# Two query groups of the second attention moved between the last projection blocks; both key halves from one product

## The chip, the cores and the metric

The kernel runs on one core of one Trainium2 chip. The metric is the device time of one execution in microseconds (us). An execution is a little longer than its span, which runs from the first to the last instruction of the profile. TensorE is called PE here, VectorE DVE, ScalarE ACT, GpSimd POOL, and SyncE (SP) is the queue from which nearly all DMAs are issued.

## What is computed

The reference is two transformer blocks in sequence on x of 2048 rows by 1024.

```
h  = rms_norm(x) * (1 + scale) + shift;  qa ka va fa za qb kb vb zb = h @ w_in
oa = forgetting_attention(8 heads of 64);  ob = sliding_window(rope(qb), rope(kb), 2 key heads)
x  = x + gate * rms_norm([oa * silu(za), ob * silu(zb)] @ w_out)
# second block, 16 meta tokens ahead of the sequence
q_a c_kv q_idx k_idx w_idx gate_a q_h f_h i_h gate_h = h @ w_in_2
a  = attention over the 256 best keys by an index score + the meta tokens, 8 heads, relative bias
r  = hgrn2(q_h, f_h, i_h)                  # recurrence over chunks of the sequence
y  = [a * silu(gate_a), rms_norm(r) * silu(gate_h)] @ w_out_2
out = layer_norm(2**0.25 * h + y)
```

## The kernel before

Products are made in float16 with a high and a low part (three products for one), and the program is written in a framework that orders the instructions of every engine ahead of time: program order gives each a priority, which `high_priority(offset=...)` shifts (a negative offset makes it less urgent), and a later instruction may be placed ahead of an earlier one that isn't ready. Once placed, every engine and the SP queue run their instructions in that order, each waiting in turn. Pools of tiles lie on a left or a right stack in SBUF; a pool that opens where another has closed waits, tile by tile, until the old tiles there have been read.

- `blocks1` makes the first projection. For the sliding keys and queries `rotated` computes, for each of 4 groups of 512 rows, two products `p[0]` and `p[1]` (the two halves of each head, m columns each; m is 64 for the keys `kb` and 128 for `qb`), and rotates them with DVE, POOL and ACT (L516 to L527). The first attention's heads run at the same time.
- `phase_proj2` makes the second projection (L1242 to L1444): index scores, latent keys and values, then the twelve blocks of `BLK2` in `stream`, where the weights of the next block are loaded and split while the current one is computed. A block `qa`, `qh` or `fh` is 8 banks of 24 products of 512 columns; a block `ga`, `gh` or `ih` 16 banks of 24 products of 256. Each bank is evacuated by ACT: Sigmoid for `fh`, Silu for `gh`, `ga` and `qh`, a copy for `qa` and `ih`. `bank()` hands out the PSUM banks in turn. `Quick.run` selects the 256 keys of each row, in three batches of row tiles (`QUICK`), on DVE and ACT, from scores in a tile `sc`, and writes the masks.
- `phase_dsa` (L1982 to L2225) then runs the second attention by query groups g of 512 rows: 8 heads each, and per head `prepare` (loads, row maxima from L2052 and L2058) and `main` (4g+4 key blocks and the meta block: products L2103 to L2115, then Exp, cast and subtraction in `Att.weights`, L746 to L752, then the products with the values, L776 to L778, three for each of the query tiles). Between the heads stand, by a count of key blocks `done`, the eight chunks of the recurrence (`CH`, `Hgrn.chunk`, one after another through single buffers) and the output product with the norm of each of 16 row tiles (`O2`, `out2`, `norm2`).

Group 0 has 5 steps a head, group 1 has 9, group 2 has 13 and group 3 has 17: 40, 72, 104 and 136 for eight heads, 352 in all.

## Time and profile before

| what | value |
|---|---|
| median of 3 runs | 3169.38 us (3162.87 to 3175.8) |
| profiled execution: time, span | 3170.48 us, 3168.7 us |
| mean granted TensorE clock | 0.938 of full speed |
| busy: PE, DVE, ACT, POOL | 2822.7, 2101.6, 1686.9, 1450.2 us |
| matmuls | 25152 |

A busy PE need not be at its peak, as matmuls overlap and their ends are modelled; where a product's price is wanted, the distance from one start to the next is read. The granted clock is given as a share of 2.4 GHz. Idle time of an engine that isn't the bound costs nothing.

### The profile page before, as it was taken

What the parts mean: (1) busy time and instruction counts of PE and PEld (TensorE: products, weight loads), DVE (VectorE), ACT (ScalarE), POOL (GpSimd) and SP (SyncE); (2) the same over time, 40 slices, a digit from 0 to 9 for tenths busy, and PEclk for the clock granted to TensorE, in tenths of its full rate; (3) what the DMA queues carried; (4) which work ended last, traced back from release to release, by engine and by line L of the source; (5) the groups of instructions that cost most, each with busy time, mean ns of one, the idle gap of its engine ahead of it and who ended that gap; (6) DMA issues with size and microseconds to landing.
All of it is one profiled execution on the core that took longest, in us unless ns stands there. A gap on an engine that the chain in (4) does not pass through costs nothing. (4 is left out here: it accounts for less than half of the span.)

```text
span 3168.7 us, 65862 instructions
## 1 busy us (share of the span) xinstructions
PE 2822.7 (89%) x25152; PEld 1858.8 (59%) x25152; DVE 2101.6 (66%) x5073; ACT 1686.9 (53%) x3058; POOL 1450.2 (46%) x1241
## 2 busy tenths in 40 slices
PE   7899999999997899999998889899678888988997
PEld 5554444477884555544445665358566566666663
DVE  7523765566678676646499699830578778888763
ACT  4423665576566655634356466321455456657763
POOL 3211446564333555534233433610456567768752
PEclk9899999999996799999999989899679989999998
DMA  6222343532235343334433532222753444443331
GB/s 235 82 87 84 105 129 111 173 95 69 79 94 167 109 142 108 124 91 157 111 97 101 160 125 73 89 91 63 182 159 102 137 133 113 118 117 110 122 97 59
DMA packets 271184, 364.28 MB, mean 115 GB/s; under 512 B 60205, under 2 KB 192033, under 8 KB 269705
## 3 DMA queue, kind: packets, MB, share of 16 engines
q1 hardware_dynamic: 270424, 359.96, 37.8%
q8 instruction: 199, 3.26, 0.4%
q14 instruction: 129, 1.05, 0.1%
q10 hardware_dynamic: 432, 0.02, 0.0%
HBM read 247.05 MB, written 112.82 MB: 114 GB/s over the span
## 5 line engine op out<-in xcount | busy, mean ns | idle before, releaser
L752 POOL TENSOR_TENSOR plo<-p,phi 128x512 f16<-128x512 f32 (+3 forms) x600 | 664.9, 1121 | 569.9 <-ACT phi L748 360.0
L748 ACT CAST phi<-p 128x512 f16<-128x512 f32 (+3 forms) x649 | 347.0, 554 | 84.2 <-PE po L778 75.1
L746 ACT ACTIVATE p<-pst,shift,dci 128x512 f32<-128x512 f32 (+4 forms) x352 | 247.4, 716 | 137.2 <-POOL plo L752 46.7
L778 PE MATMUL po<-v,plo 128*128 128x65 f16 x2176 | 270.1, 196 | 35.0 <-POOL plo L752 27.9
L776 PE MATMUL po<-v,phi 128*128 128x65 f16 x2176 | 286.4, 197 | 5.3 <-ACT phi L748 4.2
L777 PE MATMUL po<-v,phi 128*128 128x64 f16 x2176 | 285.3, 198 | 0.0
L778 PEld LDWEIGHTS <-plo 128*128 128x128 f16 x2424 | 234.7, 101 | 79.2 <-POOL plo L752 46.8
L746 ACT ACTIVATE p<-pst,shift,fci 128x512 f32<-128x512 f32 (+1 forms) x320 | 220.1, 710 | 113.1 <-PE pst L984 70.2
L963 DVE TENSOR_REDUCE mu<-p 128x1 f32<-128x512 f32 (+2 forms) x320 | 188.4, 603 | 130.1 <-PE p L959 83.3
L776 PEld LDWEIGHTS <-phi 128*128 128x128 f16 x2424 | 236.1, 100 | 48.8 <-ACT phi L748 11.4
L284 POOL TENSOR_TENSOR wlo<-wraw,whi 128x512 f16<-128x512 f32 (+3 forms) x116 | 149.9, 1310 | 216.9 <-ACT whi L283 214.0
L2058 DVE CUSTOM_DVE_ANT_0 jk<-p,mk 128x512 bf16<-128x512 f32 (+2 forms) x320 | 193.4, 604 | 80.5 <-PE p L2052 32.8
L777 PEld LDWEIGHTS <-phi 128*128 128x128 f16 x2424 | 235.6, 100 | 15.3 <-issue 1.8
L337 PE MATMUL pp<-whi,hhi 128*128 128x256 f16 (+2 forms) x824 | 235.0, 286 | 7.7 <-ACT whi L283 5.7
L339 PE MATMUL pp<-whi,hlo 128*128 128x256 f16 (+2 forms) x824 | 233.2, 285 | 4.2 <-POOL hlo L465 4.2
L338 PE MATMUL pp<-wlo,hhi 128*128 128x256 f16 (+2 forms) x824 | 234.7, 285 | 0.6 <-POOL wlo L284 0.6
L326 PE MATMUL pp<-hhi,whi 128*128 128x512 f16 (+2 forms) x496 | 190.7, 384 | 4.4 <-DVE ra L523 4.4
L328 PE MATMUL pp<-hhi,wlo 128*128 128x512 f16 (+2 forms) x496 | 190.3, 384 | 0.0
L327 PE MATMUL pp<-hlo,whi 128*128 128x512 f16 (+2 forms) x496 | 190.0, 383 | 0.0
L328 PEld LDWEIGHTS <-wlo 128*128 128x128 f16 (+2 forms) x1000 | 99.7, 100 | 122.6 <-POOL wlo L284 10.9
L326 PEld LDWEIGHTS <-whi 128*128 128x128 f16 (+2 forms) x1000 | 100.5, 101 | 120.1 <-issue 10.2
L327 PEld LDWEIGHTS <-whi 128*128 128x128 f16 (+2 forms) x1000 | 99.9, 101 | 117.3 <-issue 16.0
(666 smaller groups left out, 8933.6 us busy)
## 6 DMA issues: line engine op xcount, KB each, us to landing
wraw<-in_w_in_dram SPq DMA_DIRECT2D x88, 256.0 KB
d_z<-er SPq DMA_DIRECT2D x128, 128.0 KB
bT<-d_rb SPq DMA_DIRECT2D x32, 384.0 KB
wa<-in_w_ada_dram SPq DMA_DIRECT2D x8, 1024.0 KB
x<-in_x_dram SPq DMA_DIRECT2D x16, 512.0 KB
d_k<-ehi SPq DMA_DIRECT2D x32, 256.0 KB
d_q<-ehi SPq DMA_DIRECT2D x32, 256.0 KB
QA<-d_q SPq DMA_DIRECT2D x64, 128.0 KB
```

The source lines that it names most:

```text
L326: nc.tensor.matmul(ps, lhsT=whi, rhs=hhi[:, kk, :], start=kk == 0, stop=False)
L327: nc.tensor.matmul(ps, lhsT=whi, rhs=hlo[:, kk, :], start=False, stop=False)
L328: nc.tensor.matmul(ps, lhsT=wlo, rhs=hhi[:, kk, :], start=False, stop=kk == KK - 1)
L337: nc.tensor.matmul(ps, lhsT=hhi[:, kk, s], rhs=whi, start=kk == 0, stop=False)
L338: nc.tensor.matmul(ps, lhsT=hhi[:, kk, s], rhs=wlo, start=False, stop=False)
L339: nc.tensor.matmul(ps, lhsT=hlo[:, kk, s], rhs=whi, start=False, stop=kk == KK - 1)
L746: nc.scalar.activation(p, s, AF.Exp, scale=ci[:m], bias=K.shift[:m])
L748: nc.scalar.copy(hi, p)
L752: e.tensor_tensor(lo, p, hi, op=ALU.subtract)
L776: nc.tensor.matmul(o, lhsT=hi, rhs=v[:, :65], start=first, stop=False, **kw)
L777: nc.tensor.matmul(o[:, 1:65], lhsT=hi, rhs=v[:, 65:129], start=False, stop=False, **kw)
L778: nc.tensor.matmul(o, lhsT=lo, rhs=v[:, :65], start=False, stop=last, **kw)
```

## The change

Two things. In `rotated`, where m is 64, one product with 128 columns of weights makes both halves in one bank, and ACT copies the upper 64 partitions to a tile `z` on the lower ones. And the heads of groups 0 and 1 leave `phase_dsa`: `attention2` is its attention code as a function of pools, `early_units` builds 16 units (group, head) with pools of its own, and `phase_proj2` calls them between blocks, 3 after each of blocks 6 to 9 and 2 after each of 10 and 11. For that the `qa` blocks come ahead of `qh`, `ga` and `ih`, and the relative bias rows and the selection come right after them in program order; the batches are cut anew (7, 4 and 3 tiles for 8, 3 and 3), and the second batch's masks are no longer put off. The pools of the selection are closed, and those of the units open in their place. The units use the banks `pt0` (2) for the scores and `psc` (2) for row maxima and sums together, where `phase_dsa` has 3, 2 and 1; the blocks keep 4 banks instead of 6. `phase_dsa` starts at group 2 with `done` at 112, and has new places for the chunks and the outputs; the extra look-ahead `NA` of the first heads is gone.

```diff
-        ("ga", [(964, 256)]), ("ga", [(1220, 256)]), ("qh", [(1476, 256)]), ("qh", [(1732, 256)]),
-        ("qa", [(0, 256)]), ("qa", [(256, 256)]), ("ih", [(2500, 256)]), ("ih", [(2756, 256)])]
+        ("qa", [(0, 256)]), ("qa", [(256, 256)]), ("qh", [(1476, 256)]), ("qh", [(1732, 256)]),
+        ("ga", [(964, 256)]), ("ga", [(1220, 256)]), ("ih", [(2500, 256)]), ("ih", [(2756, 256)])]
+
+UNITS = (3, 3, 3, 3, 2, 2)
...
-CH = [2, 20, 56, 92, 128, 164, 200, 236]
-O2 = [40 + 16 * t for t in range(4)] + [112 + 20 * t for t in range(4)] + [220 + 24 * t for t in range(4)] + [318]
+CH = [113, 135, 160, 185, 210, 235, 262, 290]
+O2 = [140, 148, 166, 174, 192, 200, 216, 224] + [240 + 20 * t for t in range(4)] + [318]
...
-QUICK = [(2, 3, 4, 5, 6, 7, 8, 9), (10, 11, 12), (13, 14, 15)]
+QUICK = [(2, 3, 4, 5, 6, 7, 8), (9, 10, 11, 12), (13, 14, 15)]
...
-                p = [ps.tile([128, 512], F32, name="pp")[:m] for _ in range(2)]
-                for a in range(2):
-                    mm3_T(K, p[a], w, a * m, h[g])
+                if m == 64:
+
+                    pb = ps.tile([128, 512], F32, name="pp")
+                    mm3_T(K, pb, w, 0, h[g])
+                    z = sp.tile([128, 512], F32, name="ra", tag="ra", bufs=4)[:m]
+                    nc.scalar.copy(z, pb[m:])
+                    p = [pb[:m], z]
+                else:
+                    p = [ps.tile([128, 512], F32, name="pp")[:m] for _ in range(2)]
+                    for a in range(2):
+                        mm3_T(K, p[a], w, a * m, h[g])
...
-                rings.extend([(pst, "st")] * EARLY + [(pst, "st"), (ps, "pp"), (psc, "psc")] * 100)
+                rings.extend([(pst, "st")] * EARLY + [(pst, "st"), (ps, "pp")] * 100)
...
-        stream(K, wp, pst, [*blocks[:4], lambda: wo_scale(K, wp, pst, A["w_out_2"], "st"), *blocks[4:10], lambda: rel_rows(K, A, sp, pt, "pt0"), *blocks[10:]], "st")
-        K.quick.run(tk, QUICK[0], 0)
-        K.quick.run(tk, QUICK[1], LATE)
-        tk2 = st.enter_context(tc.tile_pool(name="tk2", bufs=1, side="right", reuse_waits="tile"))
-        K.quick.run(tk2, QUICK[2], LATE)
+        tk = st.enter_context(ExitStack())
+        units = []
+
+        def selection():
+            t1 = tk.enter_context(tc.tile_pool(name="tk", bufs=1, reuse_waits="tile"))
+            K.quick.run(t1, QUICK[0], 0)
+            K.quick.run(t1, QUICK[1], 0)
+            t2 = tk.enter_context(tc.tile_pool(name="tk2", bufs=1, side="right", reuse_waits="tile"))
+            K.quick.run(t2, QUICK[2], LATE)
+            tk.close()
+            units.extend(early_units(K, st, (psc, "psc"), (pt, "pt0"), (psc, "psc")))
...
+        late = [x for b, n in zip(blocks[6:], UNITS) for x in (b, lambda n=n: some(n))]
+        stream(K, wp, pst, [*blocks[:4], lambda: wo_scale(K, wp, pst, A["w_out_2"], "st"), *blocks[4:6],
+                            lambda: rel_rows(K, A, sp, pt, "pt0"), selection, *late], "st")
...
+def early_units(K, sk, ps1, pst, pso):
+
+    nc, tc = K.nc, K.tc
+    left = lambda n, b: sk.enter_context(tc.tile_pool(name=n, bufs=b, reuse_waits="tile"))
+    pp, sm, wp = left("esp", 3), left("ess", 2), left("esw", 1)
+    op = sk.enter_context(tc.tile_pool(name="eso", bufs=2, side="right", reuse_waits="tile"))
+    wm = zero_tiles(K, wp)
+    at = Att(K, pp, sm, ps1[0], 1.0, 0.9, ps1[1])
+    masks, prepare, main = attention2(K, at, op, sm, wp, wm, ps1, pst, pso, 2)
+    steps = [(g, h) for g in range(2) for h in range(8)]
...
+        weave(main(g, h, ready.pop(0), mks[g]), side, *WV[1])
+
+    return [lambda i=i: unit(i) for i in range(len(steps))]
...
-        steps = [(g, h) for g in range(NG) for h in range(8)]
+        steps = [(g, h) for g in range(g0, NG) for h in range(8)]
...
-        done = 0
+        done = sum(8 * (4 * g + 5) for g in range(g0))
...
-        phase_dsa(K, A, out)
+        phase_dsa(K, A, out, 2)
```

## Rows read from the trace of the kernel before

**Rows 1.** Busy time of each engine by stretch; last granted clock, DMA share, GB/s:

```profile
420.00:500.00 80.00, 77.46 (x580) 39.71 (x579) 45.22 (x105) 45.13 (x91) 51.42 (x49) 1.00 0.39 121
1842.00:2056.00 214.00, 189.14 (x1176) 117.80 (x1174) 194.09 (x554) 115.37 (x187) 95.25 (x49) 0.93 0.26 89
2056.00:2214.00 158.00, 156.37 (x1125) 108.61 (x1123) 29.28 (x60) 38.48 (x78) 18.99 (x21) 1.00 0.25 78
2214.00:2365.00 151.00, 98.53 (x1085) 81.70 (x1084) 102.69 (x239) 73.08 (x129) 69.28 (x56) 0.71 0.68 175
2365.00:2585.00 220.00, 184.83 (x2132) 133.34 (x2130) 170.06 (x344) 117.22 (x194) 132.15 (x101) 0.90 0.43 125
2585.00:2843.00 258.00, 230.67 (x2871) 168.21 (x2871) 209.19 (x427) 161.69 (x263) 181.68 (x139) 0.95 0.39 111
2843.00:3119.00 276.00, 258.02 (x3216) 179.25 (x3211) 190.00 (x419) 191.34 (x316) 190.58 (x153) 0.99 0.34 101
3119.00:3169.00 50.00, 29.42 (x126) 12.87 (x126) 25.92 (x43) 3.38 (x6) 6.93 (x6) 0.84 0.26 93
```

**Rows 2.** One line's instructions, first and last start: selection's last reads, last projection copies:

```profile
L1786 ACT ACTIVATE jk<-sc,nt x14: 614/1306/1997, 1749.0 to 2054.9; 128x384 bf16<-128x384 f32 x1, 128x512 bf16<-128x512 f32 x1, 128x640 bf16<-128x640 f32 x1, 128x768 bf16<-128x768 f32 x1
L1404 ACT ACTIVATE er<-pp,winv x11: 474/474/474, 2135.1 to 2216.4; 128x256 f32<-128x256 f32 x11
```

**Rows 3.** Key rotation, 425 to 505: groups by shape (busy us, mean ns | idle before):

```profile
L326 PE MATMUL pp<-hhi,whi 128*64 128x512 f16 x59 | 22.6, 383 | 1.1 <-DVE ra L523 1.1
L480 ACT CAST ehi<-ra 64x512 f16<-64x512 f32 x8 | 4.9, 615 | 8.3 <-DMA d_kb<-ehi 8.1 <-POOL ra L525 0.2
```

**Rows 4.** Timeline of PE in the key rotation (start us, length us):

```profile
424.88 0.38 PE L328 MATMUL pp<-hhi,wlo 128*64 128x512 f16 x1
425.09 0.38 PE L326 MATMUL pp<-hhi,whi 128*64 128x512 f16 x1
```

**Rows 5.** Timeline of PE in the second attention, full clock:

```profile
2487.15 0.38 PE L2115 MATMUL pst<-idb,mk 128*128 128x128 bf16 x4
2487.37 0.38 PE L2103 MATMUL pst<-QA,KA 66*128 66x512 f16 x1
...
2488.03 0.19 PE L776 MATMUL po<-v,phi 128*128 128x65 f16 x1
2488.06 0.20 PE L777 MATMUL po<-v,phi 128*128 128x64 f16 x1
...
2490.76 0.58 PE L2113 MATMUL pst<-bT,jr 128*128 128x256 f32 x2
2491.18 0.23 PE L2115 MATMUL pst<-idb,mk 128*128 128x128 bf16 x1
```

**Rows 6.** Groups of DVE instructions from 2214 to 2585:

```profile
L2058 DVE CUSTOM_DVE_ANT_0 jk<-p,mk 128x512 bf16<-128x512 f32 (+2 forms) x108 | 60.3, 558 | 24.0 <-PE p L2055 11.8 <-DMA mk<-d_mask 7.1 <-PE p L2052 2.0
...
L763 DVE TENSOR_SCALAR zrow<-mx 128x4 f16<-128x4 f32 x17 | 12.4, 730 | 0.3
L789 DVE TENSOR_SCALAR r<-r,vinv 128x4 f32<-128x4 f32 x16 | 8.8, 549 | 0.2
L752 DVE TENSOR_TENSOR plo<-p,phi 128x256 f16<-128x256 f32 (+1 forms) x10 | 8.8, 876 | 1.7 <-POOL plo L752 1.1 <-ACT phi L748 0.6
L2058 DVE DVE_READ_ACCUMULATOR2_ANT mu<- 128x1 f32 x108 | 8.6, 80 | 0.0
```

**Rows 7.** The recurrence's eight results, first and last store:

```profile
L1951 SPq DMA_DIRECT2D d_a<-o x8: 359/360/370, 2347.6 to 2966.8; - x8
```

**Rows 8.** Timeline of ACT where Sin and Exp alternate:

```profile
396.48 1.28 ACT L671 ACT_TABLE_LOAD   x1
397.77 0.63 ACT L671 ACTIVATE r<-r 128x512 f32<-128x512 f32 x1
```

**Rows 9.** What the SP queue waited for, 2214 to 2585 (total us, times, longest):

```profile
SPq L379 <- PE pst L2104: 43.4, 8, 13.5
SPq L2037 <- PE p L2055: 35.8, 8, 17.1
```

More of the change, by code (lines that the diff above doesn't have):

```diff
@@ L765, in max_rows @@
         nc.vector.scalar_tensor_tensor(z[:, :, 65], z[:, :, 64], -a / b, t, op0=ALU.mult, op1=ALU.add)
-        p = self.pm.tile([128, 512], F32, name="p1")
+        p = self.pm.tile([128, 512], F32, name=self.tag)
         for s in range(4):
@@ L1436, in phase_proj2, with some @@
         blocks = [(*w2_of(A, cols), K.xinv, set2(kind, cols[0][0]), kind in ("ga", "gh")) for kind, cols in BLK2]
-        stream(K, wp, pst, [*blocks[:4], lambda: wo_scale(K, wp, pst, A["w_out_2"], "st"), *blocks[4:10], lambda: rel_rows(K, A, sp, pt, "pt0"), *blocks[10:]], "st")
-        K.quick.run(tk, QUICK[0], 0)
-        K.quick.run(tk, QUICK[1], LATE)
-        tk2 = st.enter_context(tc.tile_pool(name="tk2", bufs=1, side="right", reuse_waits="tile"))
-        K.quick.run(tk2, QUICK[2], LATE)
+        tk = st.enter_context(ExitStack())
[8 more added lines that the diff above has]
+            units.extend(early_units(K, st, (psc, "psc"), (pt, "pt0"), (psc, "psc")))
+        def some(n):
+            for _ in range(n):
+                units.pop(0)()
+        late = [x for b, n in zip(blocks[6:], UNITS) for x in (b, lambda n=n: some(n))]
+        stream(K, wp, pst, [*blocks[:4], lambda: wo_scale(K, wp, pst, A["w_out_2"], "st"), *blocks[4:6],
+                            lambda: rel_rows(K, A, sp, pt, "pt0"), selection, *late], "st")
         with tc.high_priority(offset=-300):
@@ new lines, in early_units, with unit @@
+def early_units(K, sk, ps1, pst, pso):
[7 more added lines that the diff above has]
+    steps = [(g, h) for g in range(2) for h in range(8)]
+    mks = [masks(g) for g in range(2)]
+    ready = []
+    def unit(i):
+        g, h = steps[i]
+        if not i:
+            x, side = prepare(g, h, mks[g])
+            ready.append(x)
+            weave(side, [])
+        side = []
+        if i + 1 < len(steps):
+            g1, h1 = steps[i + 1]
+            x, side = prepare(g1, h1, mks[g1])
+            ready.append(x)
+        weave(main(g, h, ready.pop(0), mks[g]), side, *WV[1])
+    return [lambda i=i: unit(i) for i in range(len(steps))]
@@ L1980, in phase_dsa, with zero_tiles @@
+def zero_tiles(K, pool):
+    wm = [pool.tile([128, 512], F16, name=f"wm{x}") for x in ("hi", "lo")]
+    for x in wm:
+        K.nc.gpsimd.memset(x, 0.0)
+    return wm
+def phase_dsa(K, A, out, g0):
     nc, tc = K.nc, K.tc
@@ L1993, in phase_dsa @@
         hg = Hgrn(K, A, st, py)
-        jr, jb = K.jr, K.jb
-        wm = [wp.tile([128, 512], F16, name=f"wm{x}") for x in ("hi", "lo")]
-        for x in wm:
-            nc.gpsimd.memset(x, 0.0)
+        masks, prepare, main = attention2(K, at, op, sm, cp, zero_tiles(K, wp), (ps1, "p1"), (pst, "pst"), (pso, "po"), NG)
         lg = os_.tile([128, D], F32, name="lg")
@@ L2002, in phase_dsa @@
         nc.sync.dma_start(lb, ap(A["ln_b"], 0, [[0, 128], [1, D]]))
-        def masks(g):
-            mk = []
-            for s in range(4):
-                i = 4 * g + s
-                m = cp.tile([128, 128 * (i % 8 + 9)], BF, name=f"mk{s}", tag=f"mk{g % 2}{s}")[:, :128 * (i + 1)]
-                if i < 2:
-                    if i:
-                        nc.vector.memset(m[:, :128], 0.0)
-                    nc.vector.tensor_copy(m[:, i * 128:], K.mR)
-                else:
-                    nc.sync.dma_start(m, K.d_mask[i * 128:(i + 1) * 128, :128 * (i + 1)])
-                mk.append(m)
-            return mk
@@ L2189, in phase_dsa @@
         fill.sort(key=lambda f: f[0])
-        mks = {g: masks(g) for g in range(2)}
+        mks = {g: masks(g) for g in range(g0, g0 + 2)}
         ready = []
@@ L2202, in phase_dsa @@
                 ready.append(x)
-            if h == MH and 0 < g < 3:
+            if h == MH and g0 < g < 3:
                 mks[g + 1] = masks(g + 1)
@@ L2258, in build @@
                     select(K, tk, b, BATCHES, 0)
-            phase_dsa(K, A, out)
+            phase_dsa(K, A, out, 0)
 def layout(i):
```

216 lines of the change are left out of this document (116 added, 100 removed).

## The prediction

> **What bounds the kernel now.** I read the table of stretches first [rows 1], cut where the program changes its work. In the key rotation (420 to 500) PE is busy 77.46 of 80 us at a granted clock of 1.00, and no other engine over two thirds: PE sets the pace there. From 1842 to 2056 the blocks `ga` and `qh` run beside the selection. DVE, which does the selection, is busy 194.09 of 214 us (91%), PE 189.14 (88%) at 0.93 of its clock. From 2056 to 2214 stand the blocks `qa` and `ih`: PE 156.37 of 158 us at full clock, DVE 29.28, ACT 38.48, POOL 18.99. Here three engines rest. Then the second attention begins, and in its first stretch, the eight heads of group 0 and the start of the recurrence, PE is busy 98.53 of 151 us at a clock of 0.71. In group 1 it is 184.83 of 220 at 0.90, in group 2 230.67 of 258 at 0.95, in group 3 258.02 of 276 at 0.99. DVE is at 68%, 77%, 81% and 69% in the four groups. The last 50 us are a tail of outputs.
>
> So the start of the attention wastes PE, just after a stretch that wasted everything else. The heads of groups 0 and 1 have short chains (score, Exp, cast, subtract, product) that leave PE waiting; a projection block is the opposite, long runs of products that wait for little. The recurrence runs through the whole attention: its first result is stored at 2347.6 and its eighth at 2966.8 [rows 7], seven intervals of 88 us on average, so it is a serial chain nearly as long as the attention itself.
>
> **Part one: both key halves from one product.** For each of 4 row groups, 48 products become 24. Starts lie 0.21 us apart [rows 4], the weights' 64 columns making no difference to that (424.88 to 425.09, 512 columns moved). 96 products fewer are 96 x 0.215 = 20.6 us of PE. Added are 4 casts or copies of 64 x 512 on ACT; a copy of that shape takes 0.615 us [rows 3], so 2.5 us of an engine busy 45 of 80 us. The new copy lies in the chain from product to rotation, but each group now needs one bank of two, so the next group's products run meanwhile; PE waited only 1.1 us for the rotation before [rows 3]. PE is 97% busy here, so most of the 20.6 us should come out of the end: I take **-16 us**. Bounds: -20.6 if all counts, and -8 if the heads that run alongside, on POOL (51 of 80 us) and DVE, hold the stretch for the rest.
>
> **Part two, the early stage.** What moves in is the attention work of 16 heads. Its PE price, from starts in [rows 4, 5]: products with values, 42 a head in group 0 and 90 in group 1, 1056 in all at 0.03 us, 32 us. Scores for the weights, 73,728 columns at 0.215 us per 512, 31 us, and 32 meta products, 7 us. Row scores, 36,864 columns, 15 us. Masks, 288 at 0.055 us, 16 us. Bias, 144 + 16 products that take 0.21 us each (two in 2490.76 to 2491.18), 34 us. Bias of the row scores, maxima and the small ones, 184 at about 0.055 and 64 shorter, some 11 us. Together **146 us**.
>
> Where can they begin? The Q, K and V tiles of the units lie on the right stack where the third batch's `sc` was. The last read of an `sc` tile starts at 2054.9 [rows 2], and DVE, at 91% until then, leaves little room to bring it forward; the product blocks add it 16 evacuations. So I expect the first unit at about 2057. By then four blocks are done, as now: `qa` and `qh` instead of `ga` and `qh`. Left are `ga` and `ih`, four blocks that take the 158 us that `qa` and `ih` take now, on PE alone. Then 158 + 146 = 304 us of PE work have to be done from 2057 on. The 26 us of PE idle ahead of 2057 stay as they are. The units need 117 us of DVE (below), and ACT has 38 of 158 us in use: both fit in 300 us. I take PE as nearly full, since whenever a unit waits, a block's products can be placed; so groups 2 and 3 start not at 2214 but at 2214 + 140 = **2354**. Bounds: +105, if the bias products cost 0.12 us (their 256 columns at the pace of [rows 4], rounded up), 14 us less, and all 27 us of idle PE time up to 2214 are filled; and +175, if PE gets no fuller than in group 1 (84%: 146/0.84).
>
> **Part three, the late stage.** `phase_dsa` now takes 3169 - 2214 = 955 us. It loses the 16 heads, but keeps all chunks, outputs and the loading of the output weights. PE: groups 2 and 3 have 489 us, the tail 29, and what comes over from the earlier stretches is some 3.5 chunks (168 products at 0.03 us and 40 of float32, some 9 us each) and 4 output tiles (48 products at 0.215 us and some transposes, 11 us each), 76 us. At 95% that is 595/0.95 = 626 us and the ramp. DVE: 102.7 + 170.1 + 209.2 + 190.0 + 25.9 = 698 us in 2214 to 3169 [rows 1]. The moved heads' share of it: the five rows of [rows 6] make 99 us (of the 108 score reductions 12 belong to group 2, 8 us less), and the other small ones 26, so 117. Left are 581 us. With 26 of them in the tail's 50 us, 555 remain, and at the 81% of group 2, the fullest stretch with all three kinds of work, 555/0.81 = 685 us. DVE is thus the later bound. With the tail of 50 and a ramp of 20 us (chosen: less than half of the 52 us that PE idled in group 0's stretch, as the early units' last heads run ahead of it) the late stage takes **755 us**. Bounds: at the 77% of group 1, 721 + 70 = 791; and 700, if the denser mixture brings DVE to 88%.
>
> The recurrence fits: eight chunks at 88 us are 704 us, and the chain can start a little ahead of 2354, as `ih` is done by then. It would be the bound at over about 90 us a chunk.
>
> **The sum**, against the profiled 3170.5 us (1.8 us over its span, and 1 us above the median): -16 + 140 - (955 - 755) = -76, that is **3094 us**.
>
> What the unit's chain costs on ACT I put at nothing beyond that, and here one more thing must be priced: `ga` and `qh` use Silu, the units Exp. A change of ACT's function table takes 1.28 us and the next activation starts 1.29 us after it began [rows 8]. Only 16 Silu evacuations of the last `ga` block, perhaps a few more, meet units; two changes each, 32 x 1.3 = 42 us of ACT in a stage where it has 100 us to spare, covered by PE's work for other banks. If the cover is gone, each evacuation is late by 2.6 us, the PE time of one bank of `ga`.
> The Trainium skill (ScalarE: Activation LUTs, What ACT_TABLE_LOAD costs) puts a switch at about 2.66 us, since it counts a drain behind the load, and its rules for kernel authors say to finish one table set before going to the next, which speaks against weaving these. The trace shows no drain here: 1.29 us. By the page's figure the 32 changes would be an estimated 85 us in place of 42, and the sum would stay, as long as they are covered.
>
> **The rivals.**
>
> *The SP queue.* It issues in order. The loads of a unit wait there for the buffers of an earlier one: the loads of Q and of the bias (`bTb`) waited 43.4 and 35.8 us in the 16 heads, at the longest 13.5 and 17.1 us [rows 9]. What stands behind them then is new: the stores of the block evacuations, of which two tiles exist, and the weights of the next block. Two tiles and four banks are six banks of 2.6 us (24 products of 256 columns at half of 0.215), 15.7 us of PE, so waits like the longest just reach through. If waits on this order, 79 us in these two groups, come to stand on PE's path, and a third as much for the other loads, 105 us as an estimate, the late stage starts at 2459 and the end is 3094 + 105 = 3199. It decides from some 76 us on. For it: the queue is one for all. Against: it needs nearly every wait to be at its worst. 9%.
>
> *The tables.* If the units start earlier than I think, beside `qh` and both `ga`, 40 Silu evacuations make 80 changes, 104 us of ACT; all on PE's path, 3198 us. For it: the list of blocks is drawn up that way. Against: `sc` isn't free. 6%.
>
> *The late stage is no denser.* Recurrence, outputs and long heads hinder each other, DVE stays at 77%, and the early stage takes +175: 3170.5 - 16 + 175 - (955 - 791) = 3166, no change. For it: no group of heads shows DVE above 81%. Against: the share is low partly because groups 0 and 1 were short of data (DMA 0.68 in group 0). 14%.
>
> *More is filled.* Early +105 and late 700: 3170.5 - 20 + 105 - 255 = 3000. For it: nearly all PE idle lies in what the change touches. 10%.
>
> *Nothing is woven.* The units stay behind the blocks and run by themselves; then 2214 plus their own pace. Their loads can start some 157 us before the blocks end, so this needs a start after 2190; 1%, and it counts as slower.
>
> **How the numbers follow.** A change of 0.5%, 16 us, is about what can be told from none. My forecast, with its own range 3035 to 3145, has 60%. Faster than 3154: 60, 10 and some 5 of the 14 where the late stage is no denser, 75%. Within 0.5%: 9%. Slower: 9 + 6 + 1, 16%. The point is 3094. The range goes from 3025, which cuts off the better half of the case where more is filled, to 3185, which takes in the undecided case and leaves out the slower ones.
>
> **What would show it.** Products of 128 weight columns alone in the key rotation, 96 fewer, and all later stages 16 us earlier. The first Exp of the second attention within 20 us of the last read of `sc`, at about 2040 with the shift; no unit instruction before. From there to the end of `ih` PE above 95% at a clock of 1.00. The first product of group 2 at about 2338; group 2 about 100 us longer than the 258 of now, with DVE at 80% or more; eight recurrence results about 88 us apart. Table loads: some 30, not 80. I am wrong if the units' Exp begins much before the selection ends, if the SP queue's waits show up as PE idle between blocks, or if DVE in the late stage falls below 77%.

## The result, and the profile after

The changed kernel takes 3262.8 us (median of 4, 3261.5 to 3267.5) against 3167.8 us for the kernel before on the same chip: ratio 1.031, 95% interval 1.028 to 1.034. It is **slower by 3.1%**; the forecast was 3094 us, 3025 to 3185. The profiled execution has a span of 3260.3 us against 3168.7, 91.6 us more.

The table of stretches of the changed kernel, columns as in [rows 1]:

```profile
420.00:500.00 80.00, 63.03 (x471) 32.74 (x470) 56.30 (x112) 47.18 (x99) 56.40 (x50) 0.89 0.38 120
2045.00:2130.00 85.00, 62.38 (x539) 49.24 (x537) 22.43 (x59) 41.52 (x65) 27.22 (x19) 0.82 0.47 106
2130.00:2340.00 210.00, 199.56 (x2141) 170.02 (x2140) 52.06 (x188) 105.97 (x196) 51.80 (x55) 1.00 0.40 102
2340.00:2473.00 133.00, 98.19 (x1057) 67.28 (x1055) 47.13 (x182) 70.33 (x126) 49.91 (x55) 0.77 0.42 122
2473.00:2735.00 262.00, 220.62 (x2757) 164.79 (x2755) 211.62 (x421) 168.36 (x274) 180.86 (x137) 0.87 0.40 117
2735.00:3117.00 382.00, 342.11 (x3946) 242.01 (x3947) 302.06 (x550) 219.78 (x349) 258.47 (x191) 0.93 0.34 103
3117.00:3260.00 143.00, 96.10 (x590) 53.90 (x589) 81.70 (x124) 19.26 (x27) 38.94 (x25) 0.83 0.25 87
```

Single lines of it, with first and last start: the selection's last reads (L1810) and the last projection copies (L1415), which answer to [rows 2]; the copy of each head's sum, once a head, for the 16 early heads (`psc`) and the 16 late ones (`po`); the loads of the recurrence's gates (L1858), and its results (L1975), which answer to [rows 7]:

```profile
L1810 ACT ACTIVATE jk<-sc,nt x14: 616/1302/2001, 1676.0 to 2044.7; 128x384 bf16<-128x384 f32 x1, 128x512 bf16<-128x512 f32 x1, 128x640 bf16<-128x640 f32 x1, 128x768 bf16<-128x768 f32 x1
L1415 ACT ACTIVATE er<-pp,winv x16: 448/473/476, 2222.8 to 2348.9; 128x256 f32<-128x256 f32 x16
L2127 ACT COPY pc<-psc x16: 355/375/376, 2108.2 to 2451.5; 128x260 f32<-128x260 f32 x16
L2127 ACT COPY pc<-po x16: 347/372/375, 2514.8 to 3116.7; 128x260 f32<-128x260 f32 x16
L1858 SPq DMA_DIRECT2D fT<-d_f x9: 359/365/371, 2460.6 to 3056.3; - x9
L1975 SPq DMA_DIRECT2D d_a<-o x8: 360/371/387, 2572.7 to 3178.5; - x8
```

The copy of each head's sum in the kernel before, all 32 heads:

```profile
L2123 ACT COPY pc<-po x32: 348/376/393, 2245.2 to 3117.3; 128x260 f32<-128x260 f32 x32
```

What the SP queue waited for from 2340 to 2480 (total us, times, longest), which answers to [rows 9]; L1846 is the recurrence's first load, of a table of constants:

```profile
SPq L381 <- PE pt L2108: 45.0, 4, 13.0
SPq L1846 <- PE psc L789: 32.2, 1, 32.2
```

Read in order of time. The key rotation has its 14 us of PE less, and nothing came of it: the first product of the index scores starts at 1398.2 (1397.5 before). The early heads begin soon after the selection's last read of `sc` (2044.7). Up to 2130 the blocks run thin (PE 62 of 85 us), then the mixture is dense: 199.56 of 210 us at full clock. But the last block is read out at 2348.9, when ten of sixteen heads are done. The other six end 17 to 19 us apart (20 to 34 before that), alone on a PE at 74% and a clock of 0.77, the last at 2451.5; the late stage's loads issue after that. The attention's last head ends at 3117, where it ended before. But the recurrence, whose results came from 2347.6 to 2966.8 [rows 7], now gives them from 2572.7 to 3178.5, and the tail is 143 us in place of 50.

In the forecast's three terms (2473 is where the first Exp of group 2 begins, so the start-up behind the last early head counts as early here): keys 0 for -16, early stage 2473 - 2214 = +259 for +140, late stage 3260 - 2473 = 787 us for 755, that is -168 for -200. 0 + 259 - 168 = +91.

### The profile page after: what moved, and what is told of

It is laid out like the page before. It is cut to its first block, busy times and chain, and to the rows that moved or that the text cites. A ratio compares the mean times of both kernels' runs of the same rounds, so it can differ in the third digit from the quotient of the medians.

```text
span 3260.3 us, 65633 instructions
## 1 busy us (share of the span) xinstructions
PE 2846.0 (87%) x25056; PEld 1865.8 (57%) x25056; DVE 2107.3 (65%) x5055; ACT 1716.6 (53%) x3084; POOL 1442.1 (44%) x1242
## 5 line engine op out<-in xcount | busy, mean ns | idle before, releaser
L789 PE MATMUL po<-v,plo 128*128 128x65 f16 x1888 | 236.8, 197 | 32.7 <-POOL plo L763 23.4
L787 PE MATMUL po<-v,phi 128*128 128x65 f16 x1888 | 250.9, 198 | 8.0 <-ACT phi L759 4.7
L788 PE MATMUL po<-v,phi 128*128 128x64 f16 x1888 | 250.9, 199 | 0.0
L757 ACT ACTIVATE p<-pst,shift,dci 128x512 f32<-128x512 f32 (+4 forms) x240 | 172.5, 731 | 86.8 <-PE pst L2119 36.4
L328 PE MATMUL pp<-hhi,whi 128*128 128x512 f16 (+1 forms) x512 | 198.1, 387 | 14.2 <-DVE wa L239 6.8
L329 PE MATMUL pp<-hlo,whi 128*128 128x512 f16 (+1 forms) x512 | 198.3, 387 | 0.0
L330 PE MATMUL pp<-hhi,wlo 128*128 128x512 f16 (+1 forms) x512 | 197.9, 387 | 0.0
L2062 DVE CUSTOM_DVE_ANT_0 jk<-p,mk 128x512 bf16<-128x512 f32 (+1 forms) x224 | 140.3, 626 | 43.9 <-PE p L2056 22.2
L329 PEld LDWEIGHTS <-whi 128*128 128x128 f16 (+1 forms) x968 | 95.9, 100 | 125.9 <-issue 28.4
L330 PEld LDWEIGHTS <-wlo 128*128 128x128 f16 (+1 forms) x968 | 96.4, 100 | 115.7 <-issue 9.0
L328 PEld LDWEIGHTS <-whi 128*128 128x128 f16 (+1 forms) x968 | 96.6, 100 | 107.4 <-issue 9.7
```

Of the source, the lines that this page charges most:

```text
L328: nc.tensor.matmul(ps, lhsT=whi, rhs=hhi[:, kk, :], start=kk == 0, stop=False)
L329: nc.tensor.matmul(ps, lhsT=whi, rhs=hlo[:, kk, :], start=False, stop=False)
L330: nc.tensor.matmul(ps, lhsT=wlo, rhs=hhi[:, kk, :], start=False, stop=kk == KK - 1)
L757: nc.scalar.activation(p, s, AF.Exp, scale=ci[:m], bias=K.shift[:m])
L787: nc.tensor.matmul(o, lhsT=hi, rhs=v[:, :65], start=first, stop=False, **kw)
L788: nc.tensor.matmul(o[:, 1:65], lhsT=hi, rhs=v[:, 65:129], start=False, stop=False, **kw)
```

## The experiments

All ratios are to the kernel before on the same chip. The changed kernel itself was timed once, ahead of the experiments; variants of it that turned out to alter nothing come out at 1.025 to 1.028, so that differences of 0.5% to its 1.031 are not read. "Without recurrence" means that each chunk's rows are a plain product of two loaded tiles.

| run | what | median us | ratio (95% interval) |
|---|---|---|---|
| | changed kernel | 3262.8 | 1.031 (1.028 to 1.034) |
| e1_keys | before + key edit | 3183.0 | 1.002 (1.0005 to 1.004) |
| e3_pc | changed, chunks more urgent | 3259.9 | 1.026 (1.023 to 1.029) |
| e4_free | changed, operand buffers moved | 3262.4 | 1.027 (1.025 to 1.029) |
| e7_free2 | the same, and scales earlier | 3266.5 | 1.028 (1.024 to 1.031) |
| e5_po | changed, `po` in another pool | 3288.5 | 1.035 (1.033 to 1.037) |
| e10_copy | changed, no Silu | 3258.5 | 1.025 (1.023 to 1.028) |
| e15_later | changed, heads a block later | 3263.4 | 1.027 (1.024 to 1.031) |
| e13_late | before, recurrence and outputs held back | 3222.3 | 1.014 (1.012 to 1.017) |
| e9a_cut | changed, 5 of 8 chunks | 3174.4 | 0.999 (0.997 to 1.001) |
| e9b_cut | before, 5 of 8 chunks | 3147.5 | 0.991 (0.988 to 0.993) |
| e11a_none | changed, without recurrence | 3049.5 | 0.961 (0.958 to 0.964) |
| e11b_none | before, without recurrence | 3014.2 | 0.949 (0.946 to 0.951) |
| e14_ten_none | 10 early heads, without recurrence | 3019.4 | 0.951 (0.947 to 0.954) |
| e8_ten | 10 early heads | 3224.4 | 1.014 (1.012 to 1.016) |
| e17_four | 4 early heads | 3205.0 | 1.010 (1.007 to 1.014) |
| e16_zero | no early head | 3220.8 | 1.013 (1.009 to 1.017) |
| e18_early | none, early stage as before | 3203.1 | 1.009 (1.006 to 1.012) |
| e19_look2 | none, look-ahead as before | 3192.3 | 1.006 (1.004 to 1.008) |

### The first four: keys, order, buffers, banks

`e1_keys` is the kernel before with the key edit alone (the `if m == 64` branch of the change).

> The kernel before with the key edit alone (both rotated halves of the 64-dimensional keys from one product). The forecast's theory, that the stretch 420 to 500 is set by TensorE: 16 us less (bounds 8 to 21), 3147 to 3160 us, ratio about 0.995, and every later stage starts 16 us earlier. The rival, that something beside the products sets where the next stage starts (in the changed kernel TensorE's busy time of 420:500 fell from 77.46 to 63.03 us, and yet its index scores start at 1398.2 against 1397.5): no change within 0.25%, 3160 to 3176 us, first index score between 1394 and 1400.

The rival held: no gain, if anything a loss of 0.2%. The first index score starts at 1402.2, a little later than either theory had it. The table of stretches of this run (columns as in [rows 1]):

```profile
420.00:500.00 80.00, 61.74 (x435) 32.05 (x433) 51.76 (x102) 42.55 (x86) 51.89 (x48) 0.85 0.39 121
```

Two forms of one line of the rotation on DVE, 425 to 510 (busy us, mean ns | idle before), input from SBUF (`ra`) and from PSUM (`pp`):

```profile
L531 DVE SCALAR_TENSOR_TENSOR ra<-ra,inv,cs 64x512 f32<-64x512 f32 x4 | 8.2, 2041 | 2.8 <-POOL ehi L481 2.8
L531 DVE SCALAR_TENSOR_TENSOR ra<-pp,inv,cs 64x512 f32<-64x512 f32 (+1 forms) x6 | 4.4, 738 | 1.5 <-PE pp L328 1.2 <-POOL ra L533 0.3
```

The same line and the next one (its twin for the other product), all operations with both inputs in SBUF, shortest, median and longest in ns:

```profile
L531 DVE SCALAR_TENSOR_TENSOR ra<-ra,inv,cs x4: 732/1184/5064, 438.6 to 487.0; 64x512 f32<-64x512 f32 x4
L532 DVE SCALAR_TENSOR_TENSOR ra<-ra,inv,cs x4: 730/804/1039, 437.9 to 480.0; 64x512 f32<-64x512 f32 x4
```

The timeline of DVE at the longest of them:

```profile
465.19 5.06 DVE L531 SCALAR_TENSOR_TENSOR ra<-ra,inv,cs 64x512 f32<-64x512 f32 x1 [2.82 <-POOL ehi L481]
470.18 1.11 DVE L773 SCALAR_TENSOR_TENSOR zrow<-zrow,t 128x4 f16<-128x4 f16 x1
```

The timeline of POOL at that time:

```profile
465.12 3.37 POOL L284 TENSOR_TENSOR wlo<-wraw,whi 128x512 f16<-128x512 f32 x3
468.45 1.25 POOL L533 TENSOR_TENSOR ra<-ra 64x512 f32<-64x512 f32 x1
```

What PE waited for from 425 to 510:

```profile
PE p L776 <- DVE zrow L773: 9.7, 2, 7.5
```

PE has 16 us less to do and waits for as much. The second half of the keys is now a copy in SBUF. Eight DVE operations read it. Most take about what those that read PSUM take (0.74 us), two on L531 take 1.64 and 5.06, and these make its average of 2.04. The worst runs just while POOL works through four operations, and the `zrow` that PE waits for stands behind it. The Trainium skill (SBUF — State Buffer, SBUF: two separate sides) says that a DVE operation with two SBUF inputs and a GpSimd operation that reads SBUF lock each other out; the two timelines agree. That this one delay eats the gain is not shown: `zrow` is 9.7 us of PE's waits, the rest are for other steps of the first attention's heads, and no run keeps the second half in PSUM.

`e3_pc`, `e4_free` and `e5_po` each loosen one thing that the profile named.

```diff
-PC, PO, Z2 = -200, -1500, 1                                     # e3_pc
+PC, PO, Z2 = 1000, -1500, 1
-    op = ...tile_pool(name="eso", bufs=2, side="right", ...)     # e4_free
+    op = ...tile_pool(name="eso", bufs=2, ...)     (and dspy opened before dsp1)
-early_units(K, st, (psc, "psc"), (pt, "pt0"), (psc, "psc"))      # e5_po
+early_units(K, st, (psc, "psc"), (pt, "pt0"), (ps, "pp"))
```

> The changed kernel with the recurrence's chunks put ahead of the attention in priority (PC from -200 to +1000); order alone, no work added or left out. Theory 1a, the recurrence of eight chunks (89 us each, back to back from 2469 to 3178) sets the end and is stretched by attention work that stands ahead of it on its engines: a chunk takes 70 to 80 us, the last result is stored 70 to 150 us earlier, and the time falls to 3160 to 3210 us. Theory 1b, the chunk's length is its own chain of dependent steps: 85 to 92 us a chunk as before, 3245 to 3275 us. Theory 2, the late stage is a matter of VectorE's and TensorE's total work and not of the recurrence: results come earlier, but the attention's last head moves back by as much, and the time stays at 3250 to 3290 us.

> The changed kernel with the early heads' operand buffers (eso) on the left side of SBUF in place of the right, and the late stage's PSUM pools opened in another order (the recurrence's two banks and the scores' first), so that masks and recurrence of the late stage wait for the last block and not for the last early head. Theory 1, the late stage is held up until 2451 by those buffers and then bounded by the recurrence's chain (about 710 us, and 82 us of outputs behind it): the first chunk starts at 2345 to 2370 and the time falls by 90 to 120 us, to 3140 to 3175. Theory 2, the work itself sets the end: in 2340 to 2473 TensorE was idle for 35 us and that is all that can be won, 3225 to 3265 us.

> The changed kernel with the early heads' result tile (po) in the pool of the blocks' second bank pair (pp) in place of the pair that their own scores use (psc). Theory 1c, the early heads are a chain held up by those two banks (23 to 30 us a head beside the blocks, 18 alone): 15 to 22 us a head, the last early head ends 30 to 80 us earlier than 2451, and the late stage moves with it, 3185 to 3235 us. Rival, TensorE is full beside the blocks (244 of 269 us busy in 2071 to 2340) and the blocks, robbed of a bank, end later: heads 23 us or more, 3250 to 3290 us.

None wins. In `e3_pc` the last result is stored at 3174.5, 4 us earlier, with 87 us from one result to the next as before: order isn't what stretches the chain. In `e4_free` one load came free (2100 in place of 2451), but the chunks' own first load and the masks still issue behind 2455, since tiles of the last scaling lay under them; so it didn't test its theory. In `e5_po` the blocks, robbed of a bank, are read out until 2446.5 in place of 2348.9, and the last early head ends at 2471.0: the rival's result.

`e7_free2` takes that hold away as well, on top of `e4_free`.

```diff
-with tc.high_priority(offset=-300):
-    prod_scale(K, sp, pt, ..., "pt0")           # behind all heads
+late.insert(8, lambda: prod_scale(K, sp, ps, ..., "pp"))   # ahead of ih
```

> The run e4_free with one more hold taken away: the scales of the last product are worked out before the last two blocks and in another PSUM pool, so that the masks of the late stage can load when the last block ends (2345) and not behind the last early head (2457). The recurrence's own tiles still overlie the early heads' buffers. Theory 1, the recurrence sets the end: its first chunk still starts at 2460 to 2480 and the time stays within 1% of the changed kernel, 3235 to 3270 us. Rival, the late stage's attention was what waited: its first Exp comes 50 us or more before 2473 and the time falls to 3150 to 3210 us.

Single lines, first and last start: the mask loads of the changed kernel, then the mask loads and the chunks' first loads of `e7_free2`:

```profile
L2020 SPq DMA_DIRECT2D mk<-d_mask x14: 319/490/1741, 2023.3 to 2459.8; - x14
L2019 SPq DMA_DIRECT2D mk<-d_mask x14: 319/432/2644, 2040.8 to 2383.0; - x14
L1857 SPq DMA_DIRECT2D fT<-d_f x9: 359/364/371, 2471.3 to 3051.0; - x9
```

The last masks now load 77 us earlier and the time does not move; the recurrence still starts at 2471, as its tiles lie under the early heads' buffers. No layout was found that frees those too, so an early recurrence beside sixteen early heads was not tried.

### Does the recurrence's place make the loss?

`e9a_cut` and `e9b_cut` leave out the last three chunks, `e11a_none` and `e11b_none` all eight.

```diff
 def chunk(self, t):
+        if t >= 5:                        # t >= 0 in e11a, e11b
+            ... load V, z; o = V * z; store o
+            return
```

> The changed kernel with the recurrence's last three chunks left out (their rows are a plain product of two loaded tiles, so the result is not the reference's there). Read beside the next run, the kernel before with the same left out. Theory 1, the recurrence's end is what holds up the end: the tail of 143 us behind the last head falls to about 50, and with some 17 us of engine work a chunk gone from beside the attention the time is 3105 to 3135 us, no more than 15 us from the next run. Theory 2, the end is set by the engines' total work and the recurrence's late end is only where it shows: 3200 to 3220 us (three chunks' work gone), 80 to 95 us above the next run.

> The kernel before with the recurrence's last three chunks left out in the same way (rows not the reference's). Both theories: the recurrence there ended 202 us before the end, so that only the work that it put beside the attention goes, some 17 us a chunk: 3105 to 3130 us.

> The changed kernel with all eight chunks of the recurrence left out (each of their rows is a plain product of two loaded tiles, so the result is not the reference's). Read beside the next run. With three chunks left out the difference of changed and before was 27 us, with none 92 to 95. Theory 1, the change loses by where the recurrence comes to lie, behind the early heads and beside groups 2 and 3 alone, and the early heads by themselves cost or win little: the difference is -15 to +15 us. Theory 2, the early heads cost more before the late stage than they save in it, whatever the recurrence does: the difference stays at +25 us or more.

> The kernel before with all eight chunks left out in the same way. Three chunks less were worth 30 us here, and the first chunks lie beside the sparse heads of groups 0 and 1: 3060 to 3115 us by both theories.

The difference of the two kernels is 95 us with eight chunks, 27 with five and 35 with none. With five chunks that is neither theory's (up to 15, or 80 to 95). With none, 35 us is above the 25 that theory 2 set itself; but its "whatever the recurrence does" is wrong, since 60 of the 95 us (51, if 1.027 is taken for the changed kernel) go with the recurrence. Both runs of the kernel before also left the ranges expected of them: 3147.5 for 3105 to 3130, and 3014.2 for 3060 to 3115. On average a chunk costs 20 us in the kernel before (1.000 - 0.949 = 5.1% for eight) and 26 to 28 in the changed one.

The averages hide the main thing. In the kernel before the first five chunks cost 0.991 - 0.949 = 4.2%, some 26 us each, and the last three 0.9%, 10 us each. In the changed kernel the first five cost 0.999 - 0.961 = 3.8%, 24 us each, and the last three 2.8 to 3.2%, 30 to 34 us each. So the first chunks were not cheap in the thin stretch of groups 0 and 1; the whole difference lies in the last three. The heads' sums show where, first the changed kernel with five chunks and its recurrence's results, then the kernel before with five:

```profile
L2135 ACT COPY pc<-po x16: 347/369/376, 2535.2 to 3112.9; 128x260 f32<-128x260 f32 x16
L1983 SPq DMA_DIRECT2D d_a<-o x5: 359/370/388, 2593.2 to 2970.9; - x5
L2131 ACT COPY pc<-po x32: 347/375/395, 2246.9 to 3086.2; 128x260 f32<-128x260 f32 x32
```

Without its last three chunks the changed kernel's last head ends 4 us earlier and its tail falls from 143 to some 71 us (span 3183.6). In the kernel before the last head comes 31 us earlier and the tail stays (54 us to the span's end at 3139.8, for 51). What the late start costs is above all the end of the chain, which runs out behind the attention.

`e13_late` asks it the other way round: no early head, no key edit, only the recurrence held back, and with it the chunks and the outputs spread as in the changed kernel.

```diff
-        hg.chunk(-1)
...
+            if i == 15:
+                hg.chunk(-1, at.on["on"])   # its first load waits for head 16
-CH = [2, 20, 56, 92, 128, 164, 200, 236]    (O2 as in the changed kernel too)
+CH = [113, 135, 160, 185, 210, 235, 262, 290]
```

> The kernel before, without early heads and without the key edit, but with the recurrence held back until the sixteenth head (its first load waits for that head's result) and its chunks and the outputs spread as in the changed kernel. Theory 1, the recurrence's late start alone makes the loss: groups 0 and 1 pass quicker (some 260 us in place of 371), the chunks all lie beside groups 2 and 3, the tail behind the last head grows from 50 to 110 us or more, and the time is 3225 to 3290 us. Theory 2, the loss is in the early heads, not in the recurrence's place: 3165 to 3195 us.

The table of stretches of `e13_late` (its profiled execution is 13 us above the median), cut at the blocks' end, the sixteenth head, the last head and the end:

```profile
2056.00:2214.00 158.00, 158.00 (x1109) 107.22 (x1108) 29.55 (x63) 40.19 (x78) 23.08 (x19) 1.00 0.22 73
2214.00:2462.00 248.00, 186.06 (x2170) 140.77 (x2168) 125.47 (x395) 150.14 (x277) 97.49 (x106) 0.82 0.61 147
2462.00:3090.00 628.00, 555.02 (x6710) 397.89 (x6710) 499.90 (x965) 379.93 (x608) 447.54 (x328) 0.93 0.37 107
3090.00:3233.00 143.00, 96.53 (x589) 54.24 (x587) 83.29 (x124) 19.18 (x26) 37.19 (x25) 0.84 0.25 87
```

Theory 1 in kind, and just short of its range (3222.3 for 3225 to 3290): +1.4%, some 45 us, half of the loss, without one early head. Compare with the changed kernel: the same tail (143 us, PE 96.5 and 96.1), nearly the same stretch for groups 2 and 3 (628 and 644). And sixteen heads that simply run behind the blocks, with no recurrence beside them, end at 2462; woven into the blocks they end at 2451.5. By these two profiled executions the weaving won 11 us.

### How many heads, and what else loses

```diff
-UNITS = (3, 3, 3, 3, 2, 2)
+UNITS = (3, 2, 2, 2, 1, 0)      # e8_ten, e14_ten_none; the rest of group 1 late
+UNITS = (1, 1, 1, 1, 0, 0)      # e17_four
+UNITS = (0, 0, 0, 0, 0, 0)      # e16_zero
+UNITS = (0, 4, 4, 4, 2, 2)      # e15_later
-AF.Silu                         # e10_copy: AF.Copy for Silu in the blocks
```

> The changed kernel with ten early heads (as many as were done when the last block ended) in place of sixteen; the other six heads of group 1 go to the late stage, and the recurrence's chunks and the outputs are spread over that again. Theory 1, the loss is that the last six heads stand between the blocks and the late stage and so the recurrence's eight chunks start 119 us late and end 62 us behind the attention: the first chunk starts at 2345 to 2365, the last result is stored before the attention's last head ends, the tail behind that head is 45 to 60 us (143 in the changed kernel), and the time is that of the kernel before within 1%, 3145 to 3195 us. Theory 2, each head brought forward costs more beside the blocks than it saves later, in proportion to their number: 10/16 of the loss stays, 3215 to 3235 us.

> The changed kernel with Copy in place of Silu where the second projection's blocks are read out (the activation itself is left out, so the result is not the reference's): ScalarE no longer changes its table between blocks and early heads. Theory 3, the 23 table loads between 2089 and 2212 and what waits behind them hold up the early heads: heads 3 us or more quicker, the last one ends 20 us or more before 2451, 3225 to 3245 us. Theory 1, the loads lie in ScalarE's idle time (139 of 269 us busy in 2071 to 2340): the last head ends between 2443 and 2455 and the time stays at 3250 to 3275 us.

> The kernel with ten early heads, with all eight chunks of the recurrence left out (rows as in the two runs before it, not the reference's). Without the recurrence sixteen early heads cost 35 us (3049.5 against 3014.2). Theory B1, that cost arises where the early heads start (TensorE idle 22 of 85 us in 2045 to 2130, since the blocks' products stand behind the first head's): it stays with ten heads, 3040 to 3060 us. Theory B2, it arises where the last six heads run alone behind the blocks (2345 to 2475, TensorE 99 of 130 us) and the late stage has to ramp up a second time: with ten it is gone, 3005 to 3025 us.

> The changed kernel with the first heads behind the second of the six blocks in place of the first (4, 4, 4, 2, 2 in place of 3, 3, 3, 3, 2, 2). Theory B1, the first head is too close to the selection's end, and TensorE stands idle behind it for 22 us: 12 to 25 us less than the changed kernel, 3235 to 3252 us. Theory B2: one or two more heads are left over when the blocks end, and the time is the same or up to 20 us more, 3258 to 3285 us.

> The changed kernel with no early head at all, and the chunks and outputs where the kernel before had them: the key edit, the block order, the selection between the blocks and the late stage's plain two-head look-ahead are left of the change. If the early heads are what loses: within 0.5% of the kernel before. If the rest of the change carries part of the loss (order of the blocks, look-ahead, key edit): 3190 us or more.

> The changed kernel with four early heads, chunks and outputs spread nearly as in the kernel before. Theory B1, the cost of starting the early heads comes with the first one: 25 us or more above the run with none. Theory B2 with the recurrence's late start: four heads push the late stage back by about 40 us and take four sparse heads out of it, 0 to 20 us above the run with none.

Busy time by stretch up to the last block's copy, in `e16_zero`:

```profile
1842.00:2244.00 402.00, 370.61 (x2474) 245.50 (x2473) 214.04 (x568) 163.87 (x292) 130.07 (x83) 0.95 0.25 81
```

The same in `e8_ten`:

```profile
1842.00:2357.00 515.00, 453.19 (x3547) 309.21 (x3545) 261.09 (x739) 266.23 (x453) 166.07 (x127) 0.94 0.34 95
```

The recurrence's gates loaded, its results, and the sums of the 22 late heads in `e8_ten`, first and last start:

```profile
L1859 SPq DMA_DIRECT2D fT<-d_f x9: 359/360/402, 2371.0 to 2931.0; - x9
L1976 SPq DMA_DIRECT2D d_a<-o x8: 359/362/387, 2477.0 to 3087.1; - x8
L2128 ACT COPY pc<-po x22: 348/376/393, 2412.2 to 3156.5; 128x260 f32<-128x260 f32 x22
```

The late stage of `e14_ten_none`, from the last early head to the last head:

```profile
2346.00:2516.00 170.00, 138.30 (x1360) 92.37 (x1359) 96.52 (x259) 86.17 (x157) 62.46 (x62) 0.89 0.81 251
2516.00:2964.00 448.00, 422.42 (x5043) 283.26 (x5041) 258.85 (x676) 306.54 (x525) 260.09 (x235) 0.99 0.37 104
```

The late stage of `e11b_none`, cut at the sixteenth head:

```profile
2214.00:2495.00 281.00, 224.92 (x2390) 162.03 (x2388) 153.75 (x437) 155.58 (x284) 109.91 (x108) 0.88 0.72 199
2495.00:2960.00 465.00, 427.87 (x5047) 287.13 (x5045) 257.17 (x676) 312.53 (x533) 260.12 (x237) 0.96 0.37 101
```

Ten heads push the blocks' end from 2244 to 2357, 113 us: 82.6 us of PE work (the forecast's price for them, 58 of 112 block steps, was 76) and 30 us of new PE idle time. Without the recurrence they give it back: late stage to the last head 618 us in place of 746, and the total is that of `e11b_none` within 0.2%. So B2 holds, not B1: the cost without recurrence comes with the last six heads (3019 to 3050), and moving the first head by a block (`e15_later`) changes nothing.

With the recurrence, ten heads end at 1.014. That is the time of theory 2 (3224.4 for 3215 to 3235), though the signs of theory 1 came in kind: the chain's first load stands at 2371.0, its last result 69 us ahead of the last head, and the tail is 69 us in place of 143. What left the tail went beside the attention, whose last head ends at 3156.5 in place of 3116.7. So with sixteen heads the tail is where the loss shows, but freeing the chain does not win all of it back. Four heads (`e17_four`) end at 1.010, none at 1.013: 16 us below the run with none, outside both of its ranges and within the noise of it, so the first heads cost nothing that can be told.

The tables cost nothing that can be measured: `e10_copy` has 1 table load in place of 23 in 2045 to 2220 and its last early head at 2449.7 in place of 2451.5.

`e16_zero` is the miss: with **no** early head it still loses 1.3%. The last two runs set one half of its remaining edits back each.

```diff
 # e18_early: selection behind the blocks, its batches and priorities as before, and
-rings.extend([(pst, "st")] * EARLY + [(pst, "st"), (ps, "pp")] * 100)
+rings.extend([(pst, "st")] * EARLY + [(pst, "st"), (ps, "pp"), (psc, "psc")] * 100)
 # e19_look2: second buffers "QA0", "KA0", "v0" for every other head of group 0, and
-            if len(ready) < 2 and i + len(ready) < len(steps):
+            if len(ready) < 2 + (i < 5) and i + len(ready) < len(steps):
```

> The run with no early head, and the early stage set back as before the change: selection behind the blocks in program order, its batches and priorities as before, and the second projection's results in three pairs of PSUM banks in place of two (the psc pair, which the early heads would need, given back). The block order, the key edit and the late stage's two-head look-ahead remain. With no early head the loss was 42 us (ratio 1.0132), and the last block ended 28 us later than in the kernel before. If those 28 us come from the selection's place and the bank pair: the last block ends 20 to 28 us earlier and the ratio falls to 1.003 to 1.008, 3185 to 3200 us. If they come from the block order or the keys: no change, 3210 to 3225 us.

> The run with no early head, and only the late stage's look-ahead set back as before the change (a third head made ready beside each of the first five, in extra buffers for every second head of group 0). In the run with none the first head's norm came 38 us behind the last block (31 in the kernel before), and the late stage took 14 us more. If the look-ahead is what the late stage lacks: 10 to 20 us less than the run with none, ratio 1.007 to 1.010. If not: within 0.3% of it, ratio 1.010 to 1.016.

The last block's copies in `e16_zero`, first and last start:

```profile
L1416 ACT ACTIVATE er<-pp,winv x16: 449/473/473, 2161.0 to 2243.7; 128x256 f32<-128x256 f32 x16
```

The same in `e18_early`:

```profile
L1416 ACT ACTIVATE er<-pp,winv x11: 474/474/475, 2145.8 to 2226.8; 128x256 f32<-128x256 f32 x11
```

The early stage's rearrangement costs 17 us at the last block, a little less than the 20 to 28 expected, and by the medians 0.4% of the time (1.013 to 1.009), which falls between the two ranges and is not clear of noise, as the intervals overlap. The missing look-ahead costs 0.8% (1.013 to 1.006, intervals apart), more than expected; the keys 0.2%. Together that is about the 1.3%. Which of the early stage's edits does it, the selection's place or the bank pair, stays open.

## Why the prediction was wrong, step by step

Two steps failed. The term of the early stage was mis-sized, by 119 of the 167 us that are missing; and "The recurrence fits" overlooked what a late start does to a serial chain.

**Keys, -16: wrong.** "Most of the 20.6 us should come out of the end" was not so: with 16 us less to do, PE waited 16 us more, in part behind a DVE operation on the copy in SBUF, in part for other steps of the first attention's heads, which are woven into this stretch.

**Where the early heads begin: nearly right.** No head runs ahead of the selection; the first table load for Exp stands at 2089.1, 44 us behind the last read of `sc` where 20 were expected. From there on 23 table loads (some 30 expected), each 1.28 us, with the next activation 1.30 us after its start as in the two lines below, and hidden (`e10_copy`). The Trainium skill (ScalarE: Activation LUTs, What ACT_TABLE_LOAD costs) puts the load alone at about 1.28 us, which the trace confirms, and a switch with its drain at 2.66, which the trace does not show. Timeline of ACT in the changed kernel, which answers to [rows 8]:

```profile
2089.14 1.28 ACT L757 ACT_TABLE_LOAD   x1
2090.44 0.77 ACT L757 ACTIVATE p<-pt,shift,dci 16x512 f32<-16x512 f32 x1
```

**Early stage, +140: mis-sized, measured +259.** "I take PE as nearly full, since whenever a unit waits, a block's products can be placed" fails at both ends. The work was priced well (82.6 us for 76), and from 2130 to 2340 PE was full. But the blocks gave out with six heads left: a head needs its own chain of steps, 20 to 34 us beside the blocks and 17 to 19 alone, while the blocks were as quick as PE let them. Those six and the start account for PE idle time of 35 and 23 us at clocks of 0.77 and 0.82. In order of time, of the 119 us some 28 stand there with no early head at all (the last block of `e16_zero` is read out at 2243.7 for 2216.4 before [rows 2]), a cost of the rearrangement for which the forecast had no term; some 30 come while ten heads and part of the next run beside the blocks (105 us from there to 2349, priced at 76); and some 54 with the last six (124 us to 2473 with the start-up behind them, priced at 70); what is left are the 6 us by which the forecast lay below its own 146 us of work, and rounding. By the runs without recurrence the last six heads cost 30 us of the total, and moving the first ones changes nothing.

**Late stage, 755 us: measured 787, and the step that failed is "The recurrence fits".** DVE's work and share were right: 595 us for 581, and 80% for 81% beside groups 2 and 3. But these groups took 644 us, where 685 and a ramp of 20 were forecast, because part of the work fell out of them into the tail (DVE 81.70 us there for 26). The tail took 143 us for 50. The forecast let the chain start a little ahead of 2354 and be done with the attention. Its gates were first loaded at 2460.6, behind the early heads' buffers, and its eight results, 87 us apart, ended 62 us behind the last head, the last chunk and the outputs of its rows with nothing beside them. More than that, the forecast took the thin stretch of groups 0 and 1 [rows 1] as waste that leaves with those heads. It was where the first three or so of the recurrence's eight results came, and what it gave was time: the chain was then done 150 us ahead of the last head, where its last three chunks cost 10 us each; started late they cost 30 to 34. Shown by `e13_late` (some 45 us, with no head moved) and by the pairs with chunks left out (51 to 60). The sign set for it failed too: group 2 did not become 100 us longer (262 us to 2735 for the 258 of before), group 3 did (382 for 276).

**The sum.** Keys 16, early stage 119, late stage 32 us worse than forecast: 167, against 3260 - 3094 = 166. The split by cause stays open, as two ways of counting the 92 to 95 us disagree. By the runs without recurrence, 5 us are for the rest of the change with ten heads, 30 for the last six heads, and the other 51 to 60 need the recurrence. By the runs with it, 42 us are there with no early head (`e16_zero`), ten heads add nothing to that (1.014), and the last six add 1.3 to 1.7%, 41 to 54 us. So what the look-ahead and the rearrangement cost depends on the recurrence, on the heads, or on both; a run with neither early heads nor recurrence would tell, and was not made. That ten early heads make the look-ahead needless would explain it, but is not shown.

**The rivals.** None was right. "The late stage is no denser" came nearest in kind, but DVE's share was not its mechanism; the tables cost nothing, and of SP's waits behind the early heads, taking away the one on the masks won nothing (`e7_free2`). The wait of the recurrence's own first loads was never taken away with sixteen heads early, so this rival is not settled for them.

No run that computes everything beats the kernel before.

## What to carry to other kernels

A thin stretch in a profile is not free to be filled or emptied before it is known what else lives in it: here it gave a serial chain its early start, and holding that chain back, without moving a head, cost half of the loss. Work brought forward into a stretch where one engine is full costs that engine's time there, so it must be repaid in full later; count also when the long work it is woven into runs out, and which buffers the next stage shares with what is then left over. Work taken off the busiest engine counts only if nothing else waits in that stretch: here TensorE had 16 us less to do and the end came no earlier.

## What was not expected of the hardware

In `e1_keys` a DVE operation of 64x512 took 0.73 to 0.75 us with one input in PSUM, each time. Of eight with both inputs in SBUF most took little more, but one took 1.64 and one 5.06 us, the latter while POOL went through four operations. The forms stand in the lines of `e1_keys` above; in the kernel before all of them read PSUM.
